# A two-layer hybrid decoder trunk: queries split on all partitions and carried by DMA, the rotary table on VectorE, and short products padded with zeros

## The chip, the cores and the metric

The kernel runs on one core of a Trainium2 chip. The metric is the device time of one execution in microseconds (us); lower is better. Three runs of the kernel before took 686.97, 687.25 and 688.60 us, a median of 687.25 us.

The engines are named as the profile names them: PE is TensorE (matmuls; PEld its weight loads), DVE is VectorE, ACT is ScalarE, POOL is GpSimd, and SP is SyncE, whose queue issues nearly all DMA transfers here.

## The reference: what is computed

Two layers work on 256 tokens of width 1024. Each layer normalises its input and makes one projection of 8224 columns, which feeds five groups of heads. Every group's output is gated, the results are laid side by side, and one output projection, normalised again, is added to the residual.

```python
for layer in range(DEPTH):                     # DEPTH = 2, SEQ = 256
    h = rms_norm(x, pre_norm[layer]) @ w_in[layer]          # 8224 columns, cut into:
    a_out = nsa_mixer(...)        # A: 8 query heads, 2 key heads; 16 compressed keys, selected and window branches
    b_out = ssd_mixer(...)        # B: chunked scan; exp of differences of cumulated log decays
    c_out = banded_attention(rope(c_q, positions), rope(c_k, positions), c_v, 127, sinks)    # C
    d_out = dilated_mixer(...)    # D: 3 patterns of 8 heads, merged by their denominators
    m_out = memory_attention(m_q, mem, m_norm[layer], m_w_kv[layer])                         # M: 256 memory rows
    mix = concat(a_out*silu(a_z), b_out, c_out*silu(c_z), d_out*silu(d_z), m_out*silu(m_z))
    x = x + rms_norm(mix @ w_out[layer], post_norm[layer])

def rope(t, positions):           # 32 frequencies
    ang = positions * inv;  cos, sin = cos(ang), sin(ang)
    return concat([t1 * cos - t2 * sin, t2 * cos + t1 * sin])
```

All inputs are float32. The kernel multiplies in a reduced form of float32 (`F32R`) and keeps the accuracy by splitting operands into a high and a low half, so that one product becomes two or three matmuls.

## The kernel before

**How the order of the work is made.** The Python code does not issue instructions. Each helper (`act`, `stt`, `ts`, `mm`, `dma` and so on, lines 451 to 563) records an operation with its engine, an estimated cost and a key, which is the matmul time recorded so far plus `self.offset`. A list scheduler (`schedule`, line 272) then plays the whole program through once, gives each operation an engine, a place in that engine's order and a buffer slot, and `emit` (line 442) writes the instructions in that order. So an edit of a cost, a key or an operation can move every instruction behind it. A smaller key means an earlier place where there is a choice. `bg` (line 876) gives a head's attention, called a unit, a key that is 15000 later than the projection beside which it is recorded. On the chip each engine takes its instructions strictly in the written order, the SP queue too.

**Projections.** A 128-column slice of the weights is loaded from DRAM into one of 5 buffers R (`w_load`, line 581), split by ACT or DVE into a high half H and by DVE into a low half L (`w_split`, line 591), and multiplied by the transposed, split input hT in 24 matmuls of 256 columns (`fm`, line 600). The DMA for the next slice can start when the R buffer's split is done. `tm` (line 621) does the same with tokens on the output rows.

**Queries.** `ev_q` (line 647) takes a finished bank of PSUM that holds two heads on 64 partitions each, scales it, and writes for each head the high half of the query on partitions 0 to 63 and the low half on partitions 64 to 127 of one page P. It needs two ACT and two DVE instructions on 64 partitions. There are 22 such banks per layer (2 for M, 4 for A, 12 for D, 4 for C), 44 in all.

**Short products.** In `unit_a` (line 1026) the values of the 16 compressed keys (`vc`) are multiplied in two matmuls whose operands have only 16 rows, once per unit, 8 times in all. In `ssd` (line 1307) `pick` and `acsT`, with 40 rows, are multiplied 16 times.

**The start.** `setup` (line 736) runs 34 matmuls on a page of ones, loads the input and the constants, and calls `setup_rope` (line 843): the angles, their reduction to one turn, and the sine are made by 14 POOL instructions (`pool`, `pool_tt`) and one ACT instruction `Sin`. Behind that stand the queries and gate of M, the compressed keys of A, and `mem_kv` (line 1404): the 256 memory rows are normalised, transposed on PE (`L462`, by the identity in `cst`) into banks, scaled and split into pages by `norm_transpose` (line 711), and multiplied by `m_w_kv`. The pages for layer 1 are stored to DRAM (`mem_d`).

## Time and profile before

| | |
|---|---|
| median of 3 runs | 687.25 us (686.97 to 688.60) |
| the profiled execution | 687.48 us; its span, from first to last instruction, 685.7 us |
| PE busy in the span | 668.2 us (97%), 5051 matmuls |
| DVE, ACT, POOL busy | 615.9 us (90%), 491.5 us (72%), 32.8 us (5%) |
| mean granted TensorE clock | 0.987 of full speed |
| DMA | 114.28 MB, 167 GB/s over the span |

A matmul's busy time overlaps the next one's, since matmuls are pipelined; how dense PE's work really is shows in the number of matmuls started in a stretch. [...]

### The profile page before, as it was taken

The page shows a single profiled execution, that of the slowest core. Times are in us where ns is not written, and L with a number is a line of the kernel's source. Part 1 is how long each engine was busy: PE and PEld are TensorE (multiplying, and loading weights), DVE is VectorE, ACT ScalarE, POOL GpSimd, SP SyncE. Part 2 cuts the span into 40 slices and gives each one's busy share as a digit, 9 for nine tenths or more (in the row PEclk, how much of TensorE's full clock was granted, in tenths as well). Part 3 has the DMA queues.
Part 4 walks back from the last instruction along what each step waited for, and adds up shares of the span by engine and source line. Part 5 has one row for each costly group of instructions (what it writes and reads, how often), then busy time and mean ns, then how long its engine had stood idle before and what let it go on. Part 6 is the DMA issues. An engine that isn't in the chain of part 4 may idle for free.

```text
span 685.7 us, 14368 instructions
## 1 busy us (share of the span) xinstructions
PE 668.2 (97%) x5051; PEld 628.3 (92%) x5051; DVE 615.9 (90%) x1777; ACT 491.5 (72%) x1230; POOL 32.8 (5%) x78
## 2 busy tenths in 40 slices
PE   8889999999999999999999999999999999999995
PEld 7879999999999998988889999899999999898884
DVE  5959899999999999998688889999999899999875
ACT  6465679997875878676476469989678677768541
POOL 2520000000000200100000000000000000000000
PEclk9978999999999999999999999999999999999998
DMA  8999652648685656545538973185967534753511
GB/s 218 253 246 277 171 152 63 185 132 233 175 227 156 180 146 199 155 124 184 159 94 234 251 202 93 32 212 140 273 158 200 164 86 125 213 154 124 171 45 62
DMA packets 163536, 114.28 MB, mean 167 GB/s; under 512 B 8694, under 2 KB 154760, under 8 KB 163464
## 3 DMA queue, kind: packets, MB, share of 16 engines
q1 hardware_dynamic: 162312, 111.26, 58.3%
q0 software_dynamic: 1152, 2.10, 1.2%
q8 instruction: 40, 0.66, 0.4%
q14 instruction: 32, 0.26, 0.1%
HBM read 110.14 MB, written 3.20 MB: 165 GB/s over the span
## 4 chain that ended last, share of the span: by engine, by line
PE 72%; DVE 17%; ACT 8%; issue 2%; DMA 0%; DVEq 0%; POOL 0%; SPq 0%; ACTq 0%; POOLq 0%
PE B L456 68%; ACT P L468 6%; PE B L462 4%; DVE P L485 4%; DVE L L485 4%; DVE P L518 3%; DVE P L522 2%; ACT H L468 2%; DVE S L518 1%; DVE P L490 1%; DVE hT_lo L518 1%; DVE x L518 0%; DVE S L490 0%; ACT L468 0%; DVE H L556 0%
## 5 line engine op out<-in xcount | busy, mean ns | idle before, releaser
L485 DVE TENSOR_TENSOR L<-R,H 128x1024 fp32r<-128x1024 f32 (+1 forms) x174 | 210.1, 1217 | 22.3 <-ACT H L468 20.1
L468 ACT ACTIVATE P<-B 64x256 fp32r<-64x256 f32 (+9 forms) x404 | 158.7, 404 | 69.6 <-PE B L456 46.0
L468 ACT ACTIVATE H<-R 128x1024 fp32r<-128x1024 f32 (+1 forms) x150 | 156.5, 1052 | 66.5 <-PE B L456 49.9
L468 ACT ACTIVATE P<-P,S 128x256 f32<-128x256 f32 (+5 forms) x262 | 112.4, 449 | 38.1 <-DVE S L531 18.2
L456 PE MATMUL B<-hT_hi,L 128*128 128x256 f32 x864 | 128.2, 284 | 3.3 <-DVE L L485 3.3
L456 PE MATMUL B<-P,P 128*128 128x256 f32 (+6 forms) x896 | 125.8, 279 | 0.7 <-DVE P L485 0.6
L456 PE MATMUL B<-hT_hi,H 128*128 128x256 f32 x864 | 124.3, 282 | 0.6 <-ACT H L468 0.6
L456 PE MATMUL B<-hT_lo,H 128*128 128x256 f32 x864 | 124.4, 281 | 0.0
L456 PEld LDWEIGHTS B<-P,P 128*128 128x128 f32 (+1 forms) x896 | 113.0, 184 | 6.0 <-ACT P L468 2.1
L456 PEld LDWEIGHTS B<-hT_hi,L 128*128 128x128 f32 x864 | 112.0, 190 | 3.8 <-DVE L L485 3.6
L456 PEld LDWEIGHTS B<-hT_hi,H 128*128 128x128 f32 x864 | 110.7, 188 | 1.8 <-ACT H L468 0.8
L456 PEld LDWEIGHTS B<-hT_lo,H 128*128 128x128 f32 x864 | 110.8, 188 | 0.1
L456 PE MATMUL B<-H,P 128*128 128x512 f32 (+1 forms) x352 | 103.3, 377 | 0.0
L485 DVE TENSOR_TENSOR P<-B,P 64x256 f32<-64x256 f32 (+5 forms) x186 | 91.6, 508 | 13.0 <-ACT P L468 10.3
L456 PEld LDWEIGHTS B<-H,P 128*128 128x128 f32 x352 | 62.1, 188 | 9.9
L456 PE MATMUL B<-L,P 128*128 128x512 f32 (+1 forms) x176 | 65.7, 373 | 0.0
L522 DVE CUSTOM_DVE_ANT_0 P<-B,P 128x128 f32<-128x128 f32 (+2 forms) x192 | 52.5, 320 | 0.6
L462 PE MATMUL B<-cst,P 128*128 128x128 f32 (+1 forms) x344 | 50.2, 276 | 1.3 <-ACT P L468 0.6
L456 PE MATMUL B<-H,hT_hi 128*128 128x256 f32 (+1 forms) x160 | 46.3, 289 | 0.0
L456 PE MATMUL B<-L,hT_hi 128*128 128x256 f32 (+1 forms) x160 | 46.2, 289 | 0.0
L456 PE MATMUL B<-H,hT_lo 128*128 128x256 f32 (+1 forms) x160 | 46.1, 288 | 0.0
L462 PEld LDWEIGHTS B<-cst,P 128*128 128x128 f32 (+1 forms) x344 | 38.3, 136 | 7.3 <-ACT P L468 2.7
(127 smaller groups left out, 703.4 us busy)
## 6 DMA issues: line engine op xcount, KB each, us to landing
R<-in_w_in_dram SPq DMA_DIRECT2D x124, 512.0 KB, 4.8
R<-in_w_out_dram SPq DMA_DIRECT2D x36, 512.0 KB, 3.8
P<-scr SPq DMA_DIRECT2D x64, 136.0 KB, 4.8
R<-in_m_w_kv_dram SPq DMA_DIRECT2D x8, 512.0 KB, 4.8
P<-in_a_cmp_w_dram SPq DMA_DIRECT2D x16, 256.0 KB, 4.8
mem_d<-P SPq DMA_DIRECT2D x8, 256.0 KB, 3.2
P<-mem_d POOLq DMA_DIRECT2D x8, 256.0 KB, 4.3
x<-in_x_dram SPq DMA_DIRECT2D x4, 256.0 KB, 3.9
```

What stands on the lines that cost most here:

```text
L456: f = lambda: self.nc.tensor.matmul(out=out.ap(), lhsT=lhsT.ap(), rhs=rhs.ap(), start=start, stop=stop)
L462: f = lambda: self.nc.tensor.transpose(out.ap(), in_.ap(), idn.ap())
L468: f = lambda: self.nc.scalar.activation(out=out.ap(), in_=in_.ap(), func=func, **{k: _ap(x) for k, x in kw.items()})
L485: f = lambda: self.nc.vector.tensor_tensor(out=out.ap(), in0=a.ap(), in1=b.ap(), op=op)
L490: return lambda: eng.tensor_scalar(out.ap(), a.ap(), _ap(s1), _ap(s2), **kw)
L518: f = lambda: self.nc.vector.scalar_tensor_tensor(out=out.ap(), in0=a.ap(), scalar=_ap(s), in1=b.ap(), op0=op0, op1=op1)
L522: f = lambda: self.nc.vector.tensor_tensor_reduce(out=out.ap(), in0=a.ap(), in1=b.ap(), scale=1.0, scalar=3e38, op0=OP.add, op1=OP.min, ac ...
```

## The change

Five edits stand in the diff.

- `ev_q` now scales and splits a whole bank on 128 partitions, with one ACT and one DVE instruction into a page `t`, and then moves the four 64-partition pieces (64 KB each) into the page `q` by four DMAs.
- `setup_rope` records its arithmetic as 11 DVE instructions instead of 14 POOL ones, with a key 80000 later (`ROPE_LATE`), and its load of the positions with it.
- `vc` has 128 rows, zero except rows 0 to 15 and 32 to 47, which both hold the 16 values; the high and low halves of the probabilities go to rows 0 to 15 and 32 to 47 of one zeroed page. One matmul of 128 rows does what two of 16 rows did.
- `pick` and `acsT` have 128 rows, the rows beyond 40 being zero; the number of matmuls stays.
- The memory's part of layer 0 gets a key 6000 earlier (`MEM0_EARLY`).

The condition added to `dma` concerns sources marked `F32R`; the new DMAs pass both sides as float32 and go to the SP queue.

```diff
@@ -49,6 +49,7 @@
 W_EARLY, DMA_EARLY, T_EARLY, ALT_LATE = 3000.0, 11000.0, 2000.0, 4000.0
 WO_ORDER = [16, 17, 0, 1, 2, 3, 12, 13, 14, 15, 4, 5, 6, 7, 8, 9, 10, 11]
 PSUM = "B"
+ROPE_LATE, MEM0_EARLY = 80000.0, 6000.0
 SOME_LATE, PE_LATE, BIAS_LATE = 40000.0, 6000.0, 3000.0
 RESERVE, MEM_EARLY = 1.0, 17000.0
 N_WARM, W_KEY = 34, 0.0
...
@@ -539,7 +532,8 @@
 
     def dma(self, out, in_, reads=(), writes=(), nbytes=None):
 
-        eng = self.nc.gpsimd if isinstance(out, V) and out.dtype == F32R else self.nc.sync
+        same = isinstance(in_, V) and in_.dtype == F32R
+        eng = self.nc.gpsimd if isinstance(out, V) and out.dtype == F32R and not same else self.nc.sync
         f = lambda: eng.dma_start(out=_ap(out), in_=_ap(in_))
         v = out if isinstance(out, V) else in_
         n = nbytes or int(np.prod(v.shape)) * 4
@@ -646,13 +640,13 @@
 
     def ev_q(self, b):
 
-        q = self.page(F32R)
-        v = q.cut(0, s=2, n=256)
+        t, q = self.page(F32R).cut(0, s=2, n=256), self.page(F32R).cut(0, s=2, n=256)
+        self.act(t[:, 0], b[:, 0:256], scale=QS)
+        self.stt(t[:, 1], b[:, 0:256], QS, t[:, 0].bitcast(F32), OP.mult, OP.subtract)
         for par in range(2):
-            self.act(v[0:64, par], b[64 * par:64 * par + 64, 0:256], scale=QS)
-        for par in range(2):
-            self.stt(v[64:128, par], b[64 * par:64 * par + 64, 0:256], QS, v[0:64, par].bitcast(F32), OP.mult, OP.subtract)
-        return v
+            for i in range(2):
+                self.dma(q[64 * i:64 * i + 64, par].bitcast(F32), t[64 * par:64 * par + 64, i].bitcast(F32))
+        return q
 
     def ev_k(self, b):
 
@@ -762,12 +756,13 @@
         self.ident_r, self.mask_r = (self.fixed([128, 128], F32R, name=n) for n in ("ident_r", "mask_r"))
         self.copy(self.ident_r.v, self.ident)
         self.copy(self.mask_r.v, self.cst[:, C_MASK:C_MASK + 128])
-        self.pick = self.fixed([40, 8], F32R, name="pick")
-        self.copy(self.pick.v, self.cst[0:40, C_E:C_E + 8])
-        self.acsT = self.fixed([40, SEQ], F32R, name="acsT")
+        self.pick = self.fixed([128, 8], F32R, name="pick")
+        self.copy(self.pick.v, self.cst[:, C_E:C_E + 8])
+        self.acsT = self.fixed([128, SEQ], F32R, name="acsT")
         self.zero(self.acsT.v)
         self.ones = self.fixed([128, 128], name="ones")
         self.zero(self.ones.v, 1.0)
+        self.offset = ROPE_LATE
         self.setup_rope()
         self.offset = -8e4
         b = self.bank()
@@ -844,32 +839,26 @@
 
         self.sc = self.fixed([128, 2, SEQ], name="sincos")
         pi = self.new("P", I32)[:, 0:SEQ]
-        off, self.offset = self.offset, SOME_LATE - DMA_EARLY
         self.dma(pi, self.bcast(self.ins["positions"], SEQ))
-        self.offset = off
         ang = self.page()[:, 0:SEQ]
-        n, r, u = (self.page()[:, 0:2 * SEQ] for _ in range(3))
-        angs = ang[:, None, :].to_broadcast([128, 2, SEQ])
+        n, r = (self.page()[:, 0:2 * SEQ] for _ in range(2))
         pair = lambda x: x.rearrange("p (s n) -> p s n", s=2)
-        self.pool(ang, pi, self.cst[:, C_INV:C_INV + 1], OP.mult)
+        self.ts(ang, pi, self.cst[:, C_INV:C_INV + 1], OP.mult)
         magic = 12582912.0
         c1 = 6.28125
         c2 = float(np.float32(np.round((2 * math.pi - c1) * 2 ** 20) / 2 ** 20))
         c3 = float(np.float32(2 * math.pi - c1 - c2))
         for i in range(2):
-            self.pool(n[:, SEQ * i:SEQ * i + SEQ], ang, float(1 / (2 * math.pi)), OP.mult, 0.25 * i, OP.add)
+            self.ts(n[:, SEQ * i:SEQ * i + SEQ], ang, float(1 / (2 * math.pi)), OP.mult, 0.25 * i, OP.add)
         for m in (magic, -magic):
-            self.pool(n, n, 1.0, OP.mult, m, OP.add)
-        for i, c in enumerate((c1, c2, c3)):
-            self.pool(u, n, -c, OP.mult, 0.0, OP.add)
-            if i:
-                self.pool_tt(r, r, u, OP.add)
-            else:
-                self.pool_tt(pair(r), angs, pair(u), OP.add)
-        self.pool(r[:, SEQ:2 * SEQ], r[:, SEQ:2 * SEQ], 1.0, OP.mult, float(math.pi / 2), OP.add)
-        self.pool(r, r, 3.1415925, OP.min, -3.1415925, OP.max)
+            self.ts(n, n, m, OP.add)
+        self.stt(pair(r), pair(n), -c1, ang[:, None, :].to_broadcast([128, 2, SEQ]), OP.mult, OP.add)
+        for c in (c2, c3):
+            self.stt(r, n, -c, r, OP.mult, OP.add)
+        self.ts(r[:, SEQ:2 * SEQ], r[:, SEQ:2 * SEQ], float(math.pi / 2), OP.add)
+        self.ts(r, r, 3.1415925, OP.min, -3.1415925, OP.max)
         self.act(self.sc.v, pair(r), AF.Sin)
-        self.pool(self.sc[:, 0], self.sc[:, 0], self.cst[:, C_SGN:C_SGN + 1], OP.mult)
+        self.ts(self.sc[:, 0], self.sc[:, 0], self.cst[:, C_SGN:C_SGN + 1], OP.mult)
         self.sinT, self.cosT = self.sc[:, 0], self.sc[:, 1]
 
 
@@ -1001,10 +990,13 @@
             self.act(vh[0:64], s, scale=0.5)
             self.act(vh[64:128], s, scale=0.5)
             self.stt(vl[0:64], s, 0.5, vh[0:64].bitcast(F32), OP.mult, OP.subtract)
-        vc = self.fixed([16, 2, 128], F32R, name=f"vc{l}").v
+        vc = self.fixed([128, 2, 128], F32R, name=f"vc{l}").v
+        self.zero(vc)
         s = b[0:16, 32:160].rearrange("p (g n) -> p g n", g=2)
-        self.act(vc[:, :, 0:64], s, scale=0.5)
-        self.stt(vc[:, :, 64:128], s, 0.5, vc[:, :, 0:64].bitcast(F32), OP.mult, OP.subtract)
+        for o in (0, 32):
+            self.act(vc[o:o + 16, :, 0:64], s, scale=0.5)
+        for o in (0, 32):
+            self.stt(vc[o:o + 16, :, 64:128], s, 0.5, vc[0:16, :, 0:64].bitcast(F32), OP.mult, OP.subtract)
         self.vc = vc
 
     def k_pages(self, n):
@@ -1066,7 +1058,6 @@
         blocks = (None, [(0, 0, 0), (1, 0, 0)], [(0, 0, 1), (0, 1, 1)], [(1, 0, 1), (1, 1, 1)])
         for n, bl in enumerate(blocks):
             bt = self.bank()
-            m = 16 if bl is None else 128
             self.begin_fuse()
             if bl is None:
                 for t in range(2):
@@ -1079,15 +1070,16 @@
                         o = 256 * i + 128 * par
                         self.tr(bt[:, o:o + 128], src(t, br, kb, par))
             self.end_fuse()
-            ph, pl = self.page(F32R), self.page(F32R)
-            self.split(ph[0:m, 0:512], pl[0:m, 0:512], bt[0:m, :])
+            ph = self.page(F32R)
             if bl is None:
+
+                self.zero(ph[:, 0:512])
+                self.split(ph[0:16, 0:512], ph[32:48, 0:512], bt[0:16, :])
                 pv = self.bank()
-                self.begin_fuse()
-                self.mm(pv[:, :], self.vc[:, g, :], ph[0:16, 0:512], start=True, stop=False)
-                self.mm(pv[:, :], self.vc[:, g, :], pl[0:16, 0:512], start=False, stop=False)
-                self.end_fuse()
+                self.mm(pv[:, :], self.vc[:, g, :], ph[:, 0:512], start=True, stop=False)
             else:
+                pl = self.page(F32R)
+                self.split(ph[:, 0:512], pl[:, 0:512], bt[:, :])
                 self.begin_fuse()
                 for i, (br, kb, t) in enumerate(bl):
                     o = pv[:, 256 * t:256 * t + 256]
@@ -1355,7 +1347,7 @@
                 self.begin_fuse()
                 for i in range(2):
                     h = 4 * g + 2 * p + i
-                    self.mm(v[:, i], self.pick[:, h:h + 1].to_broadcast([40, 128]), self.acsT.v, start=(i == 0), stop=False)
+                    self.mm(v[:, i], self.pick[:, h:h + 1].to_broadcast([128, 128]), self.acsT.v, start=(i == 0), stop=False)
                 self.mm(b.v, self.ident_r.v, self.mask_r[:, None, :].to_broadcast([128, 4, 128]), start=False, stop=True)
                 self.end_fuse()
                 for t in range(2):
@@ -1403,7 +1395,7 @@
 
     def mem_kv(self, l, after=None):
         mkv = self.ins["m_w_kv"][l]
-        self.offset = 0.0 if after is None else -MEM_EARLY
+        self.offset = -MEM0_EARLY if after is None else -MEM_EARLY
         mem = self.load_mem(l)
         self.after, self.offset = after, 0.0
         ks = [self.ev_k(self.fm(mem, (mkv, 128 * c, 128))) for c in range(2)]
```

The scheduler's order changes on every engine. The three places that matter below follow. In the names, `B` is a PSUM bank, `P` a page, `R`, `H` and `L` a weight buffer and its halves, `cst` the constants with the identity.

POOL, at the start of the program, before:

```order
L537 MEMSET P_322 128x8 x2
L537 MEMSET P_437 128x8 x2
L490 ISA
L490 TENSOR_SCALAR P_476<-P_281,cst 128x256
L490 TENSOR_SCALAR P_503<-P_476 128x256 x2
L490 TENSOR_SCALAR P_503<-P_503 128x512 x2
L490 TENSOR_SCALAR P_549<-P_503 128x512
L502 TENSOR_TENSOR P_561<-P_476,P_549 128x512
L490 TENSOR_SCALAR P_549<-P_503 128x512
L502 TENSOR_TENSOR P_561<-P_561,P_549 128x512
L490 TENSOR_SCALAR P_549<-P_503 128x512
L502 TENSOR_TENSOR P_561<-P_561,P_549 128x512
```

POOL, the same place, with the change:

```order
L530 MEMSET acsT 128x256
L530 MEMSET ones 128x128
L530 MEMSET vc_107 128x256
L530 MEMSET P_321 128x8 x2
L530 MEMSET P_375 128x512
L530 MEMSET P_453 128x8 x2
L530 MEMSET P_467 128x512
L530 MEMSET P_776 128x8 x2
L530 MEMSET P_783 128x512
```

The rotary table's arithmetic is gone from POOL; new are zeroed pages of 128x512 for the padded products and one of `vc`. The table's DVE instructions stand at places 175 to 215 of DVE's 1655 rows, behind the memory's pages and splits.

PE, the last projection rows that `tm` issues for A's values, and the transposes of the memory rows behind them (`cst`), before:

```order
L456 MATMUL B7_620<-H0_613,hT_hi_93 128x288
L456 MATMUL B7_620<-L0_630,hT_hi_93 128x288
L456 MATMUL B7_620<-H0_613,hT_lo_94 128x288
L462 MATMUL B1_684<-cst_83,P34_493 128x128 x2
L462 MATMUL B1_684<-cst_83,P38_527 128x128 x2
L462 MATMUL B2_695<-cst_83,P34_493 128x128 x2
L462 MATMUL B2_695<-cst_83,P38_527 128x128 x2
L462 MATMUL B0_705<-cst_83,P35_495 128x128 x2
L462 MATMUL B0_705<-cst_83,P39_529 128x128 x2
L462 MATMUL B3_713<-cst_83,P35_495 128x128 x2
L462 MATMUL B3_713<-cst_83,P39_529 128x128 x2
L456 MATMUL B4_721<-P19_260,rb_101 33x400
```

PE, with the change, the first part of the same `tm`:

```order
L457 MATMUL B4_587<-H2_546,hT_lo_94 128x288
L463 MATMUL B5_603<-cst_83,P35_479 128x128 x2
L457 MATMUL B6_606<-H2_546,hT_hi_93 128x288
L457 MATMUL B6_606<-L2_562,hT_hi_93 128x288
L457 MATMUL B6_606<-H2_546,hT_lo_94 128x288
L457 MATMUL B6_606<-H2_546,hT_hi_93 128x288
L457 MATMUL B6_606<-L2_562,hT_hi_93 128x288
L457 MATMUL B6_606<-H2_546,hT_lo_94 128x288
L457 MATMUL B6_606<-H2_546,hT_hi_93 128x288
L457 MATMUL B6_606<-L2_562,hT_hi_93 128x288
L457 MATMUL B6_606<-H2_546,hT_lo_94 128x288
L463 MATMUL B5_603<-cst_83,P39_526 128x128 x2
```

The sixteen transposes stood behind all 48 matmuls of that `tm`; now they stand between them, the first two after nine.

SP's queue at about the same place, before:

```order
L543 DMA rb_101<-in_rel_bias_dram 32x32
L543 DMA P21_281<-in_positions_dram 128x256
L543 DMA R0_335<-in_w_in_dram 128x8x128
L543 DMA R1_348<-in_w_in_dram 128x3x128
L543 DMA R1_348<-in_w_in_dram 128x3x152
L543 DMA R1_348<-in_w_in_dram 128x3x8
L543 DMA R2_372<-in_w_in_dram 128x3x128
L543 DMA R2_372<-in_w_in_dram 128x3x152
L543 DMA R2_372<-in_w_in_dram 128x3x8
L543 DMA R3_394<-in_w_in_dram 128x2x128
L543 DMA R3_394<-in_w_in_dram 128x2x152
L543 DMA R3_394<-in_w_in_dram 128x2x8
```

SP's queue with the change:

```order
L537 DMA R0_334<-in_w_in_dram 128x8x128
L537 DMA R1_347<-in_w_in_dram 128x3x128
L537 DMA R1_347<-in_w_in_dram 128x3x152
L537 DMA R1_347<-in_w_in_dram 128x3x8
L537 DMA R2_371<-in_w_in_dram 128x3x128
L537 DMA P24_383<-P22_367 64x256 x2
L537 DMA R2_371<-in_w_in_dram 128x3x152
L537 DMA P24_383<-P22_367 64x256 x2
L537 DMA P28_420<-P26_406 64x256 x4
L537 DMA R2_371<-in_w_in_dram 128x3x8
L537 DMA R3_474<-in_w_in_dram 128x2x128
L537 DMA R3_474<-in_w_in_dram 128x2x152
```

The load of the positions has gone, and eight DMAs of the two M queries (`P24`, `P28`) stand between the weight loads for the `tm`; each waits on the queue for the ACT or DVE instruction that makes its source.

## Rows read from the trace of the kernel before

**Rows 1.** The page: busy time of each engine, share of the span, instructions.
```profile
PE 668.2 (97%) x5051; PEld 628.3 (92%) x5051; DVE 615.9 (90%) x1777; ACT 491.5 (72%) x1230; POOL 32.8 (5%) x78
```
**Rows 2.** Windows of 20 us: busy (count) per engine, clock, DMA share, GB/s.
```profile
20.00:40.00 20.00, 17.15 (x119) 16.54 (x118) 18.07 (x37) 11.29 (x27) 12.50 (x15) 0.83 0.95 255
40.00:60.00 20.00, 17.50 (x106) 15.24 (x106) 13.05 (x28) 14.71 (x31) 1.59 (x4) 0.83 0.90 257
...
80.00:100.00 20.00, 20.00 (x174) 19.72 (x173) 19.66 (x65) 15.79 (x46) 0.52 (x1) 1.00 0.67 179
```
**Rows 3.** Timeline of the start: start, length, engine, line, operation, idle before and releaser.
```profile
30.75 1.31 POOL L502 TENSOR_TENSOR P<-P,P 128x512 f32<-128x512 f32 x1
30.87 2.27 DVE L485 TENSOR_TENSOR L<-R,H 128x1024 fp32r<-128x1024 f32 x1
...
33.19 2.07 PE L456 MATMUL B<-hT_hi,L 128*128 128x256 f32 x8 [2.85 <-DVE L L485]
...
43.61 1.28 ACT L468 ACT_TABLE_LOAD   x1
...
47.73 2.77 PE L456 MATMUL B<-P,H 128*128 128x256 f32 x7 [1.24 <-ACT P L468]
...
51.77 2.48 PE L456 MATMUL B<-P,H 128*128 128x256 f32 x9 [1.26 <-ACT P L468]
...
59.13 0.40 PE L456 MATMUL B<-H,P 128*128 128x256 f32 x2
```
**Rows 4.** Windows inside the start, columns as in rows 2.
```profile
30.10:33.20 3.10, 0.25 (x4) 0.04 (x2) 3.07 (x4) 0.00 (x0) 2.93 (x3) 0.89 1.07 290
33.20:39.00 5.80, 5.80 (x24) 5.40 (x25) 4.48 (x6) 4.30 (x10) 4.48 (x6) 0.50 0.87 241
...
46.50:51.80 5.30, 2.80 (x8) 1.54 (x8) 4.45 (x10) 5.29 (x16) 0.73 (x4) 0.79 0.46 124
51.80:56.30 4.50, 4.50 (x20) 4.40 (x21) 4.37 (x10) 4.38 (x9) 0.00 (x0) 0.50 1.04 359
```
**Rows 5.** Groups by shape: count, busy us, mean ns, idle before.
```profile
L485 DVE TENSOR_TENSOR L<-R,H 128x1024 fp32r<-128x1024 f32 x168 | 204.6, 1225 | 21.0 <-ACT H L468 18.8 <-ACT P L468 1.5
...
L518 DVE SCALAR_TENSOR_TENSOR P<-B,P 64x256 fp32r<-64x256 f32 x72 | 30.4, 423 | 1.9 <-ACT P L468 0.2
...
L518 DVE SCALAR_TENSOR_TENSOR P<-P,P 128x512 f32<-128x512 f32 x12 | 8.3, 689 | 0.0
...
L490 DVE TENSOR_SCALAR P<-P,S 128x512 f32<-128x512 f32 x3 | 3.0, 1030 | 0.0
...
L490 DVE TENSOR_SCALAR P<-x,S 128x512 f32<-128x512 f32 x3 | 1.5, 486 | 0.1
```
**Rows 6.** PE's timeline around the first `vc` product, columns as in rows 3.
```profile
109.43 0.63 PE L456 MATMUL B<-hT_hi,L 128*128 128x256 f32 x4
109.98 0.73 PE L456 MATMUL B<-P,vc 16*128 16x512 f32 x2
110.64 0.38 PE L456 MATMUL B<-P,P 128*128 128x256 f32 x1
```
**Rows 7.** PE's timeline around the first `pick` product.
```profile
257.73 0.63 PE L456 MATMUL B<-hT_lo,H 128*128 128x256 f32 x4
258.28 0.50 PE L456 MATMUL B<-acsT,pick 40*128 40x256 f32 x2
258.71 0.50 PE L456 MATMUL B<-mask_r,ident_r 128*128 128x512 f32 x1
```
**Rows 8.** PE's timeline in the output projection: products of 512 columns.
```profile
295.61 0.63 PE L456 MATMUL B<-H,P 128*128 128x512 f32 x2
...
296.31 0.40 PE L456 MATMUL B<-H,P 128*128 128x512 f32 x1
```
**Rows 9.** DMA issues: queue, count, KB each, median us from issue to landing.
```profile
R<-in_w_in_dram SPq DMA_DIRECT2D x124, 512.0 KB, 4.8
...
mem_d<-P SPq DMA_DIRECT2D x8, 256.0 KB, 3.2
```

6 lines of the change are left out of this document (removed).

## The prediction

> **What bounds the kernel now.** The first view is the page's row of busy times: PE 97% and DVE 90% of the span [rows 1]. Since matmuls overlap, I read next how many start in a stretch. From 60 us on the windows of 20 us look alike; in the one at 80 us PE starts 174 at full clock, one each 0.115 us, although DVE is busy 19.66 of its 20 us [rows 2]. There PE's own work is the bound, and an instruction saved on ACT or DVE gains nothing. The two windows from 20 to 60 us differ: 119 and 106 matmuls, and a clock of 0.83 [rows 2]. At 174 they would have needed (119 + 106) x 0.115 = 25.9 us; they took 40. So some 14 us are lost at the start.
>
> The timeline of the start and shorter windows say where. At 30 us PE runs out of work and stands 2.85 us, until DVE has split a weight buffer [rows 3]. That split took 2.27 us where its group's mean is 1.225 [rows 3, 5], and just then POOL worked on the rotary table [rows 3]; two scalings before it are in a group of 1030 ns, against 486 ns for the same shape made from `x` while POOL was idle [rows 5]. After the stall 24 matmuls take 5.8 us at half the clock [rows 4]. At 46.5 us PE waits again, now for ACT: the memory's pages are scaled only after the whole `tm`, and behind a table load for the sine [rows 3]. 8 matmuls take 5.3 us, and the 20 behind them 4.5 us at half the clock [rows 4]. In both places the clock fell after PE had been without work.
>
> **The change part by part.** The sums are made against the profiled execution, 687.48 us (span 685.7 and 1.8 around it), which is 0.23 us above the median 687.25.
>
> *The start.* Rotary table gone from POOL, sine gone from ACT, memory earlier. Take the instant 59.13 us, when the first product of the memory's values starts [rows 3]; the same product stands with the same work ahead of it in the new order. From 30.1 us on PE must still do 8 matmuls, 2 small transposes, 48 of `tm`, 16 transposes, one bias product and 48 of the memory's keys: 123 at 0.115 us are 14.1 us, so PE alone could be there at 44.3. DVE must do, from 28.6 us on, one scaling (0.5), four splits of 1024 columns (4.9), two of 864 and one of 576 (2.8 by size), four copies (1.2; 0.3 each, an estimate from 0.42 at twice the width), and 17 scalings or splits of the memory's pages and two of A's values of 0.42 each (8.0, by the mean of the 64x256 group, since all have 256 columns): 17.4 us, so 46.0 by the durations of [rows 5]. The two are so close that some waiting must stay: transposes, ACT's pages, DVE's pages and PE's products follow one another in small steps. DMA limits too: from 20 to 60 us it moved 255 and 257 GB/s with shares of 0.95 and 0.90 [rows 2], 10.2 MB, not all of it needed by then, and the two M queries add 0.5 MB. If all had to come by then at 290 GB/s, the rate of the window at 30 us [rows 4], it would be 20 + 10.7/0.29 = 57 us. The ends are a gain of 59.1 - 46.0 = 13.1 and of 59.1 - 57 = 2. I take 49 us, a gain of 10.0, nearer to the engines: between 46.5 and 51.8 us the DMA share is 0.46 [rows 4], so the loads were ahead of their use.
>
> [...]
>
> *The short products.* Four full matmuls before a `vc` pair take 0.55 us from first start to the pair's start, where 4 x 0.115 is 0.46: 0.09 lost on entering. The pair takes 0.66 us, to 110.64 [rows 6], where two products of 512 columns cost 0.47 at the rate of three in 0.70 us [rows 8]: 0.19 lost inside it and on leaving. With the change there is one product of 0.233 us and, since all have 128 rows, no such loss: 0.233 + 0.09 + 0.19 = 0.51 us saved, 8 times, 4.1 us. A `pick` pair enters with 0.09 lost and takes 0.43 us [rows 7] where two of 256 columns are 0.23: 0.29 saved, 8 times, 2.3 us; the count of matmuls stays. PE is the bound around both (109 and 258 us), so this goes to the end in full: 6.4 us. The lower end is that zero rows cure nothing: 8 x 0.233 = 1.9 us. Below that is excluded, for a product's time in this trace goes by its columns, and these stay. The zeroed pages are POOL's, busy 5% [rows 1].
>
> [...]
>
> *The queries.* For each of the 44 banks one ACT and one DVE instruction go: DVE loses 44 x 0.423 = 18.6 us of work [rows 5], ACT about as much. PE does not wait for either past 60 us, so I count nothing. What they add is 176 DMAs on SP and a later query. A store of a page, the nearest row, takes 3.2 us to land [rows 9]; with two instructions ahead and four issues a query is some 6 us late. The order shows what hides that: between the last matmul of a query's bank and the first one that reads the query stand at least 84 matmuls in layer 0 and in layer 1 (A's second query), 84 x 0.115 = 9.7 us. If that cover failed, each of the 44 would cost up to 6 - 2 = 4 us. For C's eight the rotation is ahead of them, and the distances from their bank are still over 12 us of matmuls.
>
> *The rotary table on DVE* costs 3 instructions at 689 ns, 3 at 486 and 5 of half that width, at most 486 [rows 5]: 5 to 6 us, beside attention of layer 0 where DVE is 98% busy [rows 2]. Hidden by what the queries give back there (four have passed by then, 1.7 us) and by units that are due late; without cover 6 us.
>
> *New waits.* SP takes its queue in order, so a weight load now stands behind queries that wait for ACT and DVE. A weight buffer comes round each 5 x 24 x 0.115 = 13.8 us; less 4.8 us to land [rows 9] and 2.5 for its two halves at 1.225 [rows 5], 6.5 us are to spare. I put 1.0 us on what slips through.
>
> Sum: 687.48 - 10.0 - 6.4 + 1.0 = 672.1, and 0.23 less against the median: about 672.
>
> **The rivals.**
> - *The start stays slow.* The engines' chain and the DMA share (0.95) are both nearly full, and eight DMAs go ahead of `tm`'s last loads. If PE still idles long enough to drop its clock once, 3 us are gained instead of 10: 679. For it: rows 2's DMA; against: the DMA share of 0.46 at 46.5 us [rows 4]. Chance 0.2.
> - *Padding brings only the removed products*, if the loss in rows 6 and 7 comes from something else than the row count: 672 + 4.5 = 676.5. For it: the pair's inner loss, which no change of shape explains; against: the same loss at 16 and at 40 rows, and not at 128. Chance 0.1.
> - *More than the sum*: the whole 13.1 us and no new waits, 668. Chance 0.08.
> - *Slower: the SP queue.* Place: each query's DMAs, which wait in front of a weight load. If the 6.5 us to spare are already used by buffers that are freed late, PE stalls for the rest of a query's way, say 0.7 us for each of 44: from 0.4 us a query (15.4 / 44) the gain is eaten, and at 0.7 x 44 = 31 us the time is 703. For it: one queue carries all; against: in the order the nearest use is 84 matmuls away, and the DMA share is 0.67 where DVE is fullest [rows 2]. Chance 0.04.
> - *The change does not do what it says*: the queries' DMAs go to SP as float32 and the order shows all 176, so only the queries' part is without effect on the end, which the forecast already has.
>
> **How the numbers follow.** The forecast of 672 has chance 0.58, with its own range 667 to 677. For 8 in 10 the range takes in the slow start and the padding that does little, and the better case: 665 to 681. Left out are the slower rival and worse mixtures. About 0.3% (2 us) is what a measurement can tell from no change. Faster by more: 0.58 + 0.2 + 0.1 + 0.08 = 0.96, less 0.01 for mixtures; slower 0.04; the same 0.01.
>
> **What would show it.** In the profile after: no POOL arithmetic before 60 us and the splits there at 1.2 us; no PE stall near 30 us, clock 1.00 from 20 to 60 us, some 150 matmuls or more in each of these windows; the memory's values started at about 49 us. 8 products of `vc`, each as far from its neighbour as any of 512 columns. Past 60 us as many matmuls per window as before. It would be wrong if PE waited for queries or weights in layer 0's attention, with the clock falling there, or if the start still showed 0.50 for some us.

## The result, and the profile after

The changed kernel takes 675.75 us (median of 4 runs, 674.92 to 677.86), the kernel before 687.92 us beside it (4 runs, 686.97 to 688.65). The ratio is 0.9828 with a 95% interval of 0.9801 to 0.9856. The forecast was 672, the range 665 to 681. The sum came out near the truth, but four of its terms did not, and their errors cancel in part.

The profile is of the run of 677.86 us, the slowest of the four. From its page, the busy times that answer to [rows 1], and the group of the queries' DMAs (count, KB each, median us to landing):

```profile
PE 658.2 (97%) x5043; PEld 625.7 (93%) x5043; DVE 593.4 (88%) x1754; ACT 474.1 (70%) x1180; POOL 23.4 (3%) x74
...
P<-P SPq DMA_DIRECT2D x176, 64.0 KB, 3.9
```

DVE is 22.5 us less busy and ACT 17.4. Where the time went is read from four stretches, by starts of PE's products in each profile: to the product of the memory's values that [rows 3] show at 59.13; from there to the last product of layer 0's output projection; from there to the first product on layer 1's input; and from there to the last product of all (the last ones are those with a high half of the weights). The product at 59.13 is by the trace the third of the values: the first starts 0.24 us earlier, in the other kernels below 0.2 to 0.8. The mark is kept, since the sum was made with it.

| us (of the profiled execution) | to the values | rest of layer 0 | transition | layer 1 |
|---|---|---|---|---|
| before | 59.1 | 291.4 | 15.3 | 311.5 |
| changed | 52.2 | 292.5 | 15.3 | 307.7 |
| difference | -7.0 | +1.1 | 0 | -3.8 |

So the start gave 7 us, layer 1 nearly 4, and the rest of layer 0, where half of the padding's gain was to come, is longer than before. First one more window of the kernel before, then windows of the changed kernel, columns as in [rows 2]:

```profile
100.00:120.00 20.00, 20.00 (x168) 19.37 (x167) 19.45 (x93) 18.71 (x69) 0.52 (x1) 1.00 0.26 68
```

```profile
20.00:40.00 20.00, 19.64 (x161) 19.16 (x159) 14.36 (x42) 12.95 (x31) 1.33 (x6) 1.00 0.79 207
40.00:60.00 20.00, 17.85 (x119) 16.34 (x120) 16.18 (x42) 12.69 (x29) 1.09 (x2) 0.83 1.11 332
...
80.00:100.00 20.00, 20.00 (x172) 19.72 (x171) 18.75 (x64) 15.11 (x38) 0.00 (x0) 1.00 0.77 201
100.00:120.00 20.00, 17.20 (x135) 16.80 (x134) 18.08 (x80) 19.66 (x63) 0.52 (x1) 0.91 0.49 119
...
30.00:35.00 5.00, 5.00 (x43) 5.00 (x42) 1.88 (x4) 1.47 (x3) 0.52 (x1) 1.00 0.45 91
...
39.50:42.20 2.70, 0.20 (x2) 0.09 (x2) 2.66 (x8) 2.70 (x8) 0.00 (x0) 0.98 1.16 298
42.20:47.00 4.80, 4.80 (x16) 3.29 (x17) 4.80 (x10) 3.86 (x9) 0.00 (x0) 0.50 1.13 324
```

From 20 to 40 us PE starts 161 products where it started 119: the stall at 30 us is gone. From 40 to 60 there is a stall again, of 2.5 us, and half clock behind it (0.50 from 42.2 to 47.0; the traces of both kernels hold no level of the clock but 1.00 and 0.50, so 0.91 is a mean). And there is a new hole: from 100 to 120 us 135 products instead of 168, at 0.91.

**The stall at 39.5 us.** The timeline of SP's queue, ACT and PE (columns as in [rows 3]), with the first product of the values as its last row:

```profile
20.00 4.01 SPq L537 DMA_DIRECT2D R<-in_w_in_dram  x5
24.10 1.33 SPq L537 DMA_DIRECT2D P<-P  x2
...
26.16 4.06 SPq L537 DMA_DIRECT2D P<-P  x6
30.27 3.61 SPq L537 DMA_DIRECT2D R<-in_w_in_dram  x4
...
35.66 0.68 ACT L469 ACTIVATE H<-R 128x576 fp32r<-128x576 f32 x1 [2.30 <-DMA R<-in_w_in_dram]
...
42.15 1.22 PE L457 MATMUL B<-P,H 128*128 128x256 f32 x4 [2.50 <-DVE P L511]
...
52.17 0.40 PE L457 MATMUL B<-H,P 128*128 128x256 f32 x2
```

The eight DMAs of the two M queries hold SP from 24.1 to 30.2 us, with one load between them; SP's waits in that stretch are 1.2 us for ACT and DVE and 0.5 for a weight load to land, and the rest is mostly its own time on them, 0.46 to 0.59 us for each at which it did not wait. The last four loads of `tm` leave only behind them, the DMA share falls to 0.45 from 30 to 35 us, and ACT waits 2.3 us for the last slice. By this chain the values come late; the run with these DMAs behind the loads, below, tests it.

**The stall at 101 us.** The sine and what stands around it:

```profile
99.01 1.28 ACT L469 ACT_TABLE_LOAD   x1
...
100.31 0.63 ACT L469 ACTIVATE sincos<-P 128x512 f32<-128x512 f32 x1
100.96 1.28 ACT L469 ACT_TABLE_LOAD   x1
100.98 0.35 DVE L491 TENSOR_SCALAR sincos<-sincos,cst 128x256 f32<-128x256 f32 x1 [1.34 <-ACT sincos L469]
...
102.84 1.22 DVE L486 TENSOR_TENSOR L<-R,H 128x1024 fp32r<-128x1024 f32 x1
...
104.11 1.22 PE L457 MATMUL B<-hT_hi,L 128*128 128x256 f32 x4 [2.80 <-DVE L L486]
```

The late table brings its sine, with a table load before and after it, into attention: 3.2 us of ACT in the stretch where ACT and DVE are fullest (18.71 and 19.45 us of 20 in the row of before). DVE waits for it ahead of a weight split, PE waits 2.80 us for the split, and the clock falls (0.91 from 100 to 120 us).

**The padded products**, to be held against [rows 6, 7]:

```profile
111.86 0.28 PE L457 MATMUL B<-H,hT_lo 128*128 128x256 f32 x1
111.98 0.40 PE L457 MATMUL B<-P,vc 128*128 128x512 f32 x1
112.21 0.64 PE L457 MATMUL B<-P,P 128*128 128x256 f32 x4
...
121.58 0.63 PE L457 MATMUL B<-hT_hi,H 128*128 128x256 f32 x4
122.31 0.50 PE L457 MATMUL B<-P,vc 128*128 128x512 f32 x1
122.65 0.77 PE L457 MATMUL B<-P,P 128*128 128x256 f32 x2
...
255.08 0.63 PE L457 MATMUL B<-hT_hi,L 128*128 128x256 f32 x4
255.54 0.40 PE L457 MATMUL B<-acsT,pick 128*128 128x256 f32 x2
255.78 0.39 PE L457 MATMUL B<-mask_r,ident_r 128*128 128x512 f32 x1
```

A `pick` pair now takes 0.24 us and loses nothing at its edges. The first `vc` product does so too (0.12 in, 0.23 on). The second one does not: 0.73 us after the start of four products that need 0.46, and 0.34 to the next.

### The profile page after: what moved, and what is told of

Read it like the earlier page. It is cut to its first block, busy times and chain, and to the rows that moved or that the text cites. A ratio compares the mean times of both kernels' runs of the same rounds, so it can differ in the third digit from the quotient of the medians.

```text
span 676.1 us, 14725 instructions
## 1 busy us (share of the span) xinstructions
PE 658.2 (97%) x5043; PEld 625.7 (93%) x5043; DVE 593.4 (88%) x1754; ACT 474.1 (70%) x1180; POOL 23.4 (3%) x74
## 4 chain that ended last, share of the span: by engine, by line
PE 67%; DVE 14%; ACT 7%; DMA 5%; SPq 4%; issue 2%; DVEq 0%; ACTq 0%
PE B L457 64%; ACT P L469 6%; DVE P L486 4%; SPq L537 4%; DMA R<-in_w_in_dram 3%; PE B L463 3%; DVE L L486 3%; DVE P L511 2%; DVE P L515 2%; DVE S L511 1%; DMA P<-in_mem_dram 1%; ACT H L469 1%; DVE P L491 1%; DMA P<-scr 1%; DVE x L511 0%
## 5 line engine op out<-in xcount | busy, mean ns | idle before, releaser
L486 DVE TENSOR_TENSOR L<-R,H 128x1024 fp32r<-128x1024 f32 (+1 forms) x174 | 209.8, 1210 | 33.9 <-ACT H L469 30.9
L469 ACT ACTIVATE H<-R 128x1024 fp32r<-128x1024 f32 (+2 forms) x156 | 163.3, 1055 | 77.5 <-PE B L457 48.8
L469 ACT ACTIVATE P<-B 64x256 f32<-64x256 f32 (+10 forms) x364 | 143.7, 408 | 65.1 <-PE B L457 46.9
L469 ACT ACTIVATE P<-P,S 128x128 f32<-128x128 f32 (+5 forms) x256 | 111.3, 453 | 33.9 <-DVE S L524 17.1
L463 PE MATMUL B<-cst,P 128*128 128x128 f32 (+1 forms) x344 | 48.5, 275 | 1.2 <-DVE P L491 1.0
```

Of the source, the lines that this page charges most:

```text
L463: f = lambda: self.nc.tensor.transpose(out.ap(), in_.ap(), idn.ap())
L469: f = lambda: self.nc.scalar.activation(out=out.ap(), in_=in_.ap(), func=func, **{k: _ap(x) for k, x in kw.items()})
L486: f = lambda: self.nc.vector.tensor_tensor(out=out.ap(), in0=a.ap(), in1=b.ap(), op=op)
```

## The experiments

The medians of the kernel before on the chips used lie from 687.3 to 687.9 us; runs of one kernel spread by 1 to 6 us, so a difference of 1 us between two kernels tells nothing. Each kernel's ratio is to the kernel before on its own chip. The stages are those of one profiled run of each kernel, which lies up to 2.3 us from its median.

| kernel | median us | ratio (95%) | to the values | rest of layer 0 | transition | layer 1 |
|---|---|---|---|---|---|---|
| before | 687.92 | 1 | 59.1 | 291.4 | 15.3 | 311.5 |
| padding alone | 684.78 | 0.9966 (0.9941 to 0.9990) | 61.2 | 289.4 | 15.3 | 310.8 |
| queries alone | 681.91 | 0.9922 (0.9895 to 0.9949) | 56.1 | 291.1 | 15.2 | 309.6 |
| all but the queries | 680.93 | 0.9920 (0.9895 to 0.9946) | 47.9 | 297.1 | 15.3 | 310.6 |
| changed | 675.75 | 0.9828 (0.9801 to 0.9856) | 52.2 | 292.5 | 15.3 | 307.7 |
| table at 180000 | 674.57 | 0.9823 (0.9792 to 0.9854) | 52.7 | 288.3 | 18.2 | 307.5 |
| table on POOL at 180000 | 677.42 | 0.9861 (0.9831 to 0.9891) | 52.1 | 290.5 | 16.7 | 307.9 |
| sign before sine | 677.14 | 0.9847 (0.9811 to 0.9882) | 51.5 | 291.5 | 15.2 | 308.1 |
| M queries' DMAs later | 672.89 | 0.9791 (0.9759 to 0.9823) | 47.7 | 291.9 | 15.3 | 307.6 |
| both mended | 671.68 | 0.9771 (0.9740 to 0.9802) | 48.2 | 289.0 | 16.7 | 307.3 |
| both, DVE's work back | 673.72 | 0.9793 (0.9763 to 0.9823) | 49.2 | 292.1 | 15.3 | 306.6 |
| both, ACT's work back | 672.07 | 0.9761 (0.9728 to 0.9795) | 48.9 | 290.3 | 18.2 | 306.8 |
| both, no padding | 674.52 | 0.9812 (0.9782 to 0.9841) | 47.6 | 291.0 | 15.2 | 310.4 |
| both, memory not early | 674.38 | 0.9806 (0.9778 to 0.9835) | 52.8 | 289.1 | 15.3 | 307.5 |

**The table later.**

```diff
-ROPE_LATE, MEM0_EARLY = 80000.0, 6000.0
+ROPE_LATE, MEM0_EARLY = 180000.0, 6000.0
```

> The changed kernel with the key of the rotary table 100000 later (180000 instead of 80000), so that its instructions and the sine stand near 200 us instead of near 100 us; the first use of the table is at 252 us. My theory: the PE stall of 2.8 us at 101 us in the changed kernel, and the half clock behind it, come from the table (two table loads and the sine are 3.2 us of ACT, and DVE, in order, waits 1.3 us for the sine ahead of a weight split that PE needs). At 200 us DVE is busy 16.5 to 17.8 us of 20 and not 18 to 19.7, so there is no stall: about 672 against 675.75 us, and the window from 100 to 120 us starts some 168 matmuls instead of 135. Rival: the table costs its 3 to 4 us wherever it stands, the stall goes with it: 676, and a loss near 200 us. Second rival: the stall at 101 us has other causes (order of attention and weights) and stays: 676, with the stall at 101 us.

The stall at 101 us went: windows of this kernel,

```profile
100.00:120.00 20.00, 20.00 (x168) 19.64 (x168) 19.62 (x83) 18.87 (x61) 0.63 (x2) 1.00 0.80 211
...
340.00:360.00 20.00, 18.04 (x128) 16.91 (x128) 19.45 (x57) 17.05 (x37) 1.04 (x2) 0.91 0.45 116
```

with 168 products and 288.3 instead of 292.5 us for the rest of layer 0. That shows the table as the cause of that hole, 4.2 us in this pair of profiles. But 2.9 us of it come back as a new wait at the transition (clock 0.91 from 340 to 360 us), and the median is only 1.2 us lower, within the spread. The second rival (other causes at 101 us) has fallen. Of the first rival, that the table costs as much wherever it stands, little is seen near 200 us: 168 products from 200 to 220 us where the changed kernel starts 175, under 1 us. The wait at the transition does not go with the key alone: of the seven kernels with the key 180000 four have it (16.7 to 18.2 us) and three do not (15.2 and 15.3); its cause stays open.

**The old queries in the changed kernel.** `ev_q` of before in its place.

```diff
-        self.act(t[:, 0], b[:, 0:256], scale=QS)
-        self.stt(t[:, 1], b[:, 0:256], QS, t[:, 0].bitcast(F32), OP.mult, OP.subtract)
...
         for par in range(2):
-            for i in range(2):
-                self.dma(q[64 * i:64 * i + 64, par]...
...
+            self.act(v[0:64, par], b[64 * par:64 * par + 64, 0:256], scale=QS)
...
+            self.stt(v[64:128, par], ...
```

> The changed kernel with the old making of the queries (two ACT and two DVE instructions of 64 partitions, no DMA). My theory: PE bounds the time past 60 us and gains nothing from the 44 instructions saved on ACT and on DVE, and loses nothing by the DMAs: 676, within 1.5 us of the changed kernel's 675.75. Rival A: the relief of DVE (18.6 us) is what hides the rotary table in attention and part of the gain: 679 to 681, with more PE waits for DVE in layer 0 and 1. Rival B: the queries' DMAs in SP's queue delay weight loads: then without them it is faster, 673 or less.

The time is 680.93 us, as rival A said, and my step on the queries fails. Without the edit the start is better by 4.3 us (values at 47.87), and the rest is worse by 4.6 in layer 0 and 2.9 in layer 1. Windows of this kernel, the first to be held against the same one of the changed kernel (0.45, 91 GB/s):

```profile
30.00:35.00 5.00, 5.00 (x43) 5.00 (x42) 3.42 (x6) 3.69 (x10) 0.00 (x0) 1.00 1.05 278
80.00:100.00 20.00, 17.30 (x143) 16.55 (x142) 18.15 (x67) 14.24 (x40) 0.00 (x0) 1.00 0.47 127
```

The stall at the sine is 5.3 us here instead of 2.8, with its table loads at 95.6 and 97.5 us; that is 2.5 of the 4.6.

**The padding alone.**

```diff
-        self.pick = self.fixed([40, 8], F32R, name="pick")
+        self.pick = self.fixed([128, 8], F32R, name="pick")
...
-        vc = self.fixed([16, 2, 128], F32R, name=f"vc{l}").v
+        vc = self.fixed([128, 2, 128], F32R, name=f"vc{l}").v
+        self.zero(vc)
```

> The kernel before with nothing but the padding (values of compressed keys in one product of 128 rows, pick and acsT with 128 rows). My theory: each of the 8 pairs loses its 0.28 us at entering and leaving and one product of 0.233, each of the 8 pick pairs 0.29: 6.4 us, so 681.5 against 687.9. Rival: only the 8 removed products count, since the loss around short products is no matter of the row count: 1.9 us, so 686.

The ratio is 0.9966, so the padding alone gives 2.3 us (0.7 to 4.1), nearer to the rival. In layer 1 only 0.7 us arrive. What PE waits for from 120 us on sums to 3.7 us in 14 waits (2.0 in 7 before); the longest two lines of that view of this kernel (engine, tile and line waited for, us, times, longest):

```profile
PE B L456 <- DVE P L485: 1.1, 3, 0.6
PE B L462 <- ACT P L468: 0.8, 4, 0.2
```

By the starts of all products of layer 1, 14 come more than 0.2 us later than the product ahead of them allows (0.117 us for 256 columns, 0.233 for 512, as such products follow one another in the trace of before), 5.5 us together; in the kernel before 7 do, 2.8 us. Without that loss layer 1 would have gained 3.4. Three of the 14 are `vc` products; most of the others are transposes. With padding and the new queries, in the changed kernel, 6 products are late, 2.6 us together; with padding and the old queries again 14, 5.4 us.

The one padded product waits for zeros, high half and low half of one page. How such a wait looks, from PE's timeline of the kernel with both places mended:

```profile
418.95 0.50 PE L457 MATMUL B<-P,vc 128*128 128x512 f32 x1 [0.21 <-DVE P L486]
419.29 0.64 PE L457 MATMUL B<-hT_hi,H 128*128 128x256 f32 x4
```

Here again 0.34 us pass to the next product instead of 0.23. By the starts in that profile seven of the eight `vc` products have such a gap behind them, and six of these seven also came late, by 0.06 to 0.37 us.

**The table on POOL, late.** `setup_rope` of before, with the key 180000.

```diff
-        self.ts(ang, pi, self.cst[:, C_INV:C_INV + 1], OP.mult)
+        self.pool(ang, pi, self.cst[:, C_INV:C_INV + 1], OP.mult)
...
+            self.pool(u, n, -c, OP.mult, 0.0, OP.add)
```

> The changed kernel with the rotary table's arithmetic back on POOL (14 instructions of before), but with the key 180000, near 200 us. My theory: DVE is slowed by POOL when both read and write at the same time, whatever the place: the weight splits that lie beside the table's POOL instructions near 200 us take about 2.2 us instead of 1.2, and scalings of 128x512 about 1.0 instead of 0.5, while the start keeps what it gained (first product of the memory's values near 52 us). The time is 672 to 676, by whether those slow splits reach PE. Rival: the slow splits of the start came from the dense DMA traffic there (0.95 of the engines), not from POOL: the splits near 200 us keep 1.2 us.

Both sides are slower beside each other, though less evenly than I said. POOL and DVE of this kernel:

```profile
186.75 2.15 POOL L503 TENSOR_TENSOR P<-P,P 128x512 f32<-128x512 f32 x1
...
186.09 1.65 DVE L486 TENSOR_TENSOR L<-R,H 128x1024 fp32r<-128x1024 f32 x1
...
190.98 1.51 DVE L486 TENSOR_TENSOR P<-P,P 128x256 fp32r<-128x256 f32 x1
```

Splits beside it take 1.45 and 1.65 us (1.21 alone), not 2.2, and others 1.20, while POOL's own products take 2.15 to 2.59 where at the start of the kernel before they took 1.28 to 1.31; one DVE instruction of 128x256 took 1.51 instead of 0.42. With a dense DMA share of 0.92 from 180 to 200 us, DMA is not ruled out as a part. The time is 677.42, above my 672 to 676 and 2.8 us above the same key on DVE, about the spread. The values start at 52.13, as in the changed kernel (52.17): what the start needs is that the table is gone from there, and not that DVE makes it.

**The M queries' DMAs behind the weight loads.** In layer 0 alone:

```diff
-    def ev_q(self, b):
+    def ev_q(self, b, late=0.0):
...
+              with self.later(late):
                 self.dma(q[64 * i:64 * i + 64, par]...
...
-            q = [self.ev_q(self.fm(h, col(M_Q + 128 * c))) for c in range(2)]
+            q = [self.ev_q(self.fm(h, col(M_Q + 128 * c)), 20000.0 if l == 0 else 0.0) for c in range(2)]
```

> The changed kernel, except that the eight DMAs of layer 0's two M queries have a key 20000 later, so that they stand on SP's queue behind the weight loads of the first tm (and behind the first load of m_w_kv) and not between them. My theory: in the changed kernel those loads waited on the queue until ACT and DVE had made the M queries (SP issued the last ones from 30.3 to 33.9 us, and the DMA share fell to 0.45 from 30 to 35 us); ACT then waited 2.3 us for the last weight slice, PE stood 2.5 us at 39.5 us and ran at half clock to 47. With the loads first this goes: the first product of the memory's values starts near 47.5 us as in the kernel with the old queries (52.2 in the changed kernel), clock 1.00 from 20 to 60 us, and the time is 671 to 672 against 675.75. Rival: the bytes of the queries or the 64-partition transfers are what slows the start, not their place: the values start at 51 to 52 us and the time is 675 to 676. Second rival: the gain at the start is lost again at the late table at 101 us: values at 47.5, time 675 or more.

SP's queue of this kernel:

```profile
19.95 6.85 SPq L537 DMA_DIRECT2D R<-in_w_in_dram  x10
...
27.41 5.73 SPq L537 DMA_DIRECT2D P<-P  x8
```

The values start at 47.69, PE does not wait from 30 to 47 us, the clock is 1.00 from 20 to 60. The same bytes in the same 64-partition pieces cost the start nothing at this place (47.87 without them): it was their place on the queue. Of the 4.5 us at the start 2.9 are in the median (672.89; all its runs lie below those of the changed kernel). The first reading is shown; its size was 1 us less.

**Both mended.** The edit above and the later table together.

```diff
-ROPE_LATE, MEM0_EARLY = 80000.0, 6000.0
+ROPE_LATE, MEM0_EARLY = 180000.0, 6000.0
...
+              with self.later(late):
```

> Both places mended at once: the M queries' DMAs behind the weight loads and the rotary table's key 180000. My theory: the two costs are apart in time and add: 4.6 us from the start and about 3.5 us from the stall at 101 us, so 667 to 670. Rival: PE that is ahead by 4.6 us meets DVE and ACT (98% busy from 100 to 160 us) earlier, and the gain is given back there: 672 to 674, with new waits for DVE or ACT between 80 and 160 us.

The time is 671.68, the lowest median here: 4 us below the changed kernel, 1.7 short of the 667 to 670. Between the two profiles, whose runs are 6.5 us apart, 4.0 are gained at the start and 3.5 in the rest of layer 0; 1.4 are given back at the transition (PE waits 1.8 us there for a page of the norm from DVE), and not between 80 and 160 us, where the rival had put it.

**The sign before the sine.**

```diff
+        self.ts(r[:, 0:SEQ], r[:, 0:SEQ], self.cst[:, C_SGN:C_SGN + 1], OP.mult)
         self.act(self.sc.v, pair(r), AF.Sin)
-        self.ts(self.sc[:, 0], self.sc[:, 0], self.cst[:, C_SGN:C_SGN + 1], OP.mult)
```

> The changed kernel with the sign of the sine put into its argument (one DVE instruction on the reduced angle, before the sine) instead of behind the sine, at the same key, so that DVE has no instruction that waits for the sine. My theory: of the 2.8 us that PE stands at 101 us, about 1.7 are DVE's wait of 1.34 us for the sine and the sign's 0.35 ahead of the weight split; they go, PE stands 1.1 us or less there, ACT's two table loads (2.6 us) and the sine stay: 673 to 675. Rival: the ACT side (3.2 us taken from the softmax of the units) is what holds DVE up: the stall stays at 2.5 us or more and the time at 675 to 676.

My theory falls, the rival holds. DVE no longer waits for the sine, and the split stands at 98.8 us; but ACT, held by table loads and sine, makes the next high half late:

```profile
97.94 1.28 ACT L469 ACT_TABLE_LOAD   x1
...
99.88 1.28 ACT L469 ACT_TABLE_LOAD   x1
...
103.26 0.17 DVE L491 TENSOR_SCALAR S<-S 128x6 f32<-128x6 f32 x1 [2.43 <-ACT P L469]
...
103.99 1.04 ACT L469 ACTIVATE H<-R 128x1024 fp32r<-128x1024 f32 x1
...
105.09 0.73 PE L457 MATMUL B<-hT_hi,H 128*128 128x256 f32 x4 [3.00 <-ACT H L469]
```

The stall is 3.0 us, the time 677.14, no better. Here DVE stands idle 2.43 us for ACT, so the table's arithmetic on DVE is not what held that product: ACT's 3.2 us in a full stretch are, and in the changed kernel DVE's wait was one of the ways by which they reached PE. What the 11 DVE instructions cost by themselves no run has tried.

**The queries alone**, in the kernel before.

```diff
+        self.act(t[:, 0], b[:, 0:256], scale=QS)
+        self.stt(t[:, 1], b[:, 0:256], QS, t[:, 0].bitcast(F32), OP.mult, OP.subtract)
...
+                self.dma(q[64 * i:64 * i + 64, par]...
```

> The kernel before with nothing but the queries by DMA. The kernel without this edit was 5.2 us slower than the changed one although its start was 4.7 us better, so the first step of my forecast (queries bring nothing past 60 us) has failed. Theory now: the saved DVE and ACT work takes away small PE waits past 120 us wherever they are; in the kernel before those waits (over 0.13 us each) sum to 5.6 us, in the kernel with padding alone to 9.9, so that it brings 1 to 3 us past 120 us here; the M queries' DMAs hold back the tm's loads at the start, which was slow already: 0 to 3 us worse. Time 685 to 688 against 687.5. Rival: the relief is worth 4.5 us in any surroundings: 683 or less.

The time is 681.91, a gain of 5.4 us by its ratio: more than my theory, as the rival said, and spread otherwise. 3.0 us are at the start (POOL's table begins at 26.0 instead of 24.4 us and the weight split starts at 28.9 instead of 30.9 and takes 1.62 instead of 2.27; the stall at 30 us is 0.8 instead of 2.85 us), 1.9 in layer 1.

**DVE's work back, ACT's work back.** One instruction per bank done twice.

```diff
+        if not late:
+            self.stt(t[0:64, 1], b[0:64, 0:256], QS, t[0:64, 0].bitcast(F32), OP.mult, OP.subtract)
```

> The kernel with both places mended (M queries' DMAs behind the weight loads, table at 180000; 671.68 us), with one DVE instruction of 64x256 done over again for each of 42 query banks (not for layer 0's M), its result overwritten, so that DVE's work is back where it was (42 x 0.42 = 17.6 us) and all else stays. My theory: the worth of the queries' edit past 60 us (5 to 7 us) is DVE's relief, since DVE is 98% busy in attention and PE's small waits are mostly for DVE: 676 to 679, with the PE waits for DVE grown. Rival: the worth lies with ACT, or with the order and the DMAs: 671 to 673 here.

```diff
+        if not late:
+            self.act(t[0:64, 0], b[0:64, 0:256], scale=QS)
```

> The same with one ACT instruction of 64x256 done over again for each of 42 query banks (42 x 0.38 = 16 us of ACT). My theory: ACT is busy 70% and gains little: 671.5 to 674. Rival: the making of high halves on ACT stands ahead of DVE's splits (DVE waits for ACT's H 28 us in all), so that ACT's relief is what counts: 676 or more. If neither this nor the run with DVE's work back is slower, the worth is one of order.

The times are 673.72 and 672.07 where the mended kernel has 671.68. The first is 2.0 us above it, between my 676 to 679 and the rival's 671 to 673: five of its six runs lie above all runs of the mended kernel (670.48 to 672.60), but the intervals of the ratios overlap, so a small cost of DVE's work is neither shown nor excluded. The second is as I expected. In layer 1 neither loses anything (306.6 and 306.8). In the rest of layer 0 the first is 3.1 us longer than the mended kernel, with a wait of 2.1 us for ACT at 206 us. The test is softer than meant: the scheduler gave other work to the other engine, so that DVE's busy time rose by 9.0 us, not 17.6, and ACT's by 9.6. So these runs do not show the 5 to 6 us of the queries' edit to be the work of one engine; since only about half of the work came back, they do not exclude it either.

**Without the padding**, in the kernel with both places mended.

```diff
-        self.pick = self.fixed([128, 8], F32R, name="pick")
+        self.pick = self.fixed([40, 8], F32R, name="pick")
...
-        vc = self.fixed([128, 2, 128], F32R, name=f"vc{l}").v
-        self.zero(vc)
+        vc = self.fixed([16, 2, 128], F32R, name=f"vc{l}").v
```

> The kernel with both places mended, without the padding (values of compressed keys in two products of 16 rows, pick and acsT with 40 rows). My theory: by the starts of the matmuls a vc pair cost 0.62 us more than one whole product and a pick pair 0.39 more, less 0.2 us for each padded vc product that waits for its operands: 3.3 + 3.1 = 6.4 us, so 678. Rival: padding alone measured only 2.5 us in the kernel before, since its products wait for DVE and POOL; if that holds here too: 674.

The time is 674.52: the padding is worth 2.8 us here, the rival's number. In layer 1 it is 3.1 (310.4 to 307.3), what I had forecast for a layer; in the rest of layer 0 2.0, and the start and the transition go the other way (0.6 and 1.5). By the starts a `vc` pair in this profile costs 0.52 us more than one whole product, not the 0.62 that I had counted, and the padded products of the mended kernel give back 0.25 each by coming late and by the gap behind them.

**The memory not early**, in the kernel with both places mended.

```diff
-ROPE_LATE, MEM0_EARLY = 180000.0, 6000.0
+ROPE_LATE, MEM0_EARLY = 180000.0, 0.0
```

> The kernel with both places mended, with the memory's part of layer 0 at its old key (MEM0_EARLY 0). My theory: the memory's pages are then scaled late again, PE waits for ACT's and DVE's pages near 42 to 48 us and its clock falls behind that wait; 3 to 5 us of the start's gain go: first product of the memory's values at 51 to 53 us, time 675 to 677. Rival: with POOL's table gone and the loads first, DVE and ACT are fast enough, and the earlier key brings nothing: values at 47 to 49, time 671 to 673.

The time is 674.38, 0.6 under my range and 1.4 above the rival's, and the values come at 52.83, as I expected: 4.6 us later, of which 2.7 arrive. PE waits (1.51 us, for ACT's high half, ahead of the product at 42.95 us) and its clock falls again, to a mean of 0.83:

```profile
40.00:60.00 20.00, 18.02 (x122) 16.84 (x121) 17.70 (x41) 11.34 (x23) 1.19 (x4) 0.83 1.07 319
```

## Why the prediction was right, and which of its steps were wrong

The time is inside the range, 3.75 us above the forecast, and the sign is right. The steps:

- *The start, 10.0 us forecast.* 7.0 in the profile. The engines could do it: where nothing stood in front of the loads the values came at 47.7 to 48.2 us, near the 46.0 that I had counted for DVE. What failed is the step that the loads were ahead of their use. I listed the eight DMAs among the rivals and gave the queue 1.0 us; they cost 4.5 us at the values (52.17 against 47.69). The same pieces behind the loads cost the start nothing here (47.69 with them, 47.87 without). Whether the pieces themselves move slower than whole tiles no run isolates.
- *The short products, 6.4 us.* 2.3 alone and 2.8 in the mended kernel. The edges went as read from [rows 6, 7], for `pick` wholly: with 128 rows 0.11 to 0.12 us pass from start to start ahead of a pair, inside it and behind it, where with 40 rows 0.20 to 0.31, 0.22 and 0.21 passed. So the loss inside the pairs of before went with the row count as well. By the starts the `pick` pairs saved 2.7 us, somewhat more than the 2.3 counted, since four of the eight had entered with 0.19 lost; the `vc` pairs saved 1.6 alone and 2.1 in the mended kernel, of 4.1. What failed is "PE is the bound around both, so this goes to the end in full": a padded `vc` product needs three writers and waits for them, and PE that is ahead waits elsewhere: in layer 1, padded alone, 14 products are late instead of 7. There the padding alone brought 0.7 us, the queries alone 1.9, both 3.8.
- *The queries, nothing.* They brought 5.4 us alone, and on top of the rest 5.2 by the medians or 0.9920 - 0.9828 = 0.0092, 6.3 us, by the ratios. "PE does not wait for either past 60 us" was read from the counts of whole windows, where waits of 0.1 to 0.6 us do not show. Where the gain past the start lies (7.5 us between the two profiles) is seen in part: 2.5 us are the shorter stall at the sine, and in layer 1 fewer products come late, 14 without the edit and 6 with it, 5.4 and 2.6 us. What makes them less late stays open: about half of DVE's work put back cost 2.0 us by the medians, not clear of the noise, and about half of ACT's 0.4, so one engine's other half, order, pages or both engines together remain.
- *The rotary table on DVE, hidden.* This step failed. It counted DVE's 5 to 6 us and forgot that the sine moves with it: two table loads and the sine, 3.2 us of ACT, from a place where they delayed the memory's pages [rows 3] to the fullest stretch. It cost 4.2 us in the rest of layer 0: PE waiting in attention (2.80 us) with the clock falling (0.91), which the forecast had named as what would show it wrong. With the table later the medians gain less, 1.2 us here and 1.2 in the kernel with the M queries' DMAs later, since part comes back at the transition.
- *New waits, 1.0 us, past 60 us by weight loads.* No wait of PE for a load was found there; what the queue was seen to cost lay at the start. Past 60 us ACT and DVE do wait for weight loads, 3.0 us in five places where before they waited for none; no run shows what of that reaches PE.

Taken by these numbers some 11 us were lost against the terms (start 3, padding 4, table 4), and 6 to 7 gained (queries 5 to 6, new waits 1). That the sum is off by less than 4 us is partly luck.

## What to carry to other kernels

Here the moved sine took two table loads of 1.28 us each along, and the queries' DMAs took their place on SP's queue: list for each moved step what every engine and queue then does around it. DMAs whose results are needed later should not stand in an in-order queue ahead of loads that could go: the eight here held SP for 5.4 us, 1.2 of them waits for ACT and DVE, and cost 4.5 us at the values. Where PE is the bound by windows, still sum its waits of a few tenths of a us before an edit on another engine is costed at nothing (in layer 1 the late products here came 5.4 us late together without the queries' edit and 2.6 with it); and check edits together, since padding and queries were worth more in layer 1 together (3.8 us) than apart (0.7 and 1.9).

## What was unexpected of the hardware

In the kernel before, products of 16 and 40 rows lose about 0.1 us at every step (four `pick` pairs 0.19 on entering), also between two of the same shape: two `vc` products start 0.33 to 0.34 us apart where 512 columns of 128 rows take 0.23, two of `pick` 0.22 where 256 columns take 0.12. On-time products of 128 rows with 256 or 512 columns mostly do not lose this: in its trace they start 0.117 and 0.232 us apart in the median. Most padded `vc` products are followed by the next after 0.31 to 0.34 us instead of 0.23 (5 of 8 in the changed kernel, 7 of 8 in the mended one), mostly those that had come late; why was not tried. Where POOL and DVE worked beside each other near 190 us, with the table on POOL at 180000, single instructions took up to 2 times as long on POOL (1.28 to 2.59 us) and up to 3.6 times on DVE (0.42 to 1.51 us), unevenly; that one slows the other is not shown apart from the DMA traffic there.
